# Two-block stack: the last layer's conditioning rows move into the first block's output, and a 16x16 inverse is ranked first

## The chip, the cores and the metric

One NeuronCore of a Trainium2 chip. The metric is the device time of one execution, in microseconds (us); the time given for a kernel is the median of its runs.

## The reference

The reference runs two transformer blocks one after the other, on 512 tokens and 256 context tokens of width 1024. The **first block** has one hybrid layer: a recurrent branch (RWKV-like: a state per head is decayed and updated token by token, in both directions), a latent-attention branch (MLA), a gate, an output product with `w_out` and a final norm. The **second block** has four attention layers of three kinds (a, b, c, a). Each of them is conditioned:

```python
for i in range(DEPTH_2):
    sh, sc, gt = jnp.split(jax.nn.silu(c) @ ada_w[i] + ada_b[i], 3, axis=-1)
    shc, scc, gtc = jnp.split(jax.nn.silu(c_ctx) @ ada_w[i] + ada_b[i], 3, axis=-1)
    ...
```

`c` and `c_ctx` are one row of 1024 each, and `ada_w[i]` is 1024 x 3072, so a layer's conditioning rows are a product of two rows with 12 MB of weights. They depend on nothing that the first block computes.

## The kernel before, in words

The program is written as one Python function, and a scheduler orders it: it simulates the instructions' times, and on each engine takes next what is ready and has the highest rank. Rank follows the order in the code; what is written inside `tc.high_priority()` is ranked ahead of the rest. The order that comes out is fixed: at run time every engine, and the queue of DMA issues on SyncE (SP), goes through its list in order, and an instruction whose semaphore isn't there yet holds all behind it.

Up to 460 us the first block's projections and attention run. From 460.7 to 957 us comes the recurrence (`rwkv`): six units i = 0..5, each for two directions d, in chunks of 64 or 128 tokens. A unit has a preparation (`rw_prep`), an inversion of triangular blocks (`rw_inv`) and steps (`rw_step`). In `rw_inv` the four 16x16 diagonal blocks of each 64 are taken out into D[0] (L1783, L1785), sent through DRAM into another layout (L1796 `dd<-dg`, L1802 `U<-dd`, `t<-dd`), inverted by a substitution on VectorE (DVE) that goes through 15 steps (L1810, L1811), and sent back the same way (L1815, L1816). Matrix products of 32x32 blocks (L1826, tile `psi`) make the inverse of the larger block from them. Lines L1901 (`psc`) and L1733 (`psw`) are other small products of a unit.

Between these units **fillers** run. `fillers` makes the conditioning rows of the second block's four layers with `ada_wide`: 24 loads of 512 KB a layer (L277, tile `adw`, two buffers), each followed by two matmuls of 512 columns (L279, tile `pad`; four records a load in the trace). After every eighth load a bias is added on DVE (L287, `ad_b`) and the rows go to DRAM (L288, `mods<-ad_b`). `fills` says how many loads stand behind each turn of a unit's generators: 1, 1, 2, 2, 1, 1. All 96 loads stand between 531.6 and 889.6 us.

Then `first` makes the first block's output: `gnorm` (per-head norm and gate; L1608 loads `zt`, L1650 adds a transpose on PE, L1654 makes the low half `hl` on DVE), `product(pair)` with `w_out` in three-part float32 (L192 to L194; weight loads L407, `wr`), the residual (L1974, L1975), norms, `store` (L2004 scales X on ScalarE (ACT), L2005 stores it as `xmid`) and `prep` of the second block's first layer (L683, a scaled transpose). The first projection of the second block's layer 0 is L192 into `ps`, weights `a_w_in`.

Of the kernel before, what the change touches and what calls it, by code (L numbers as in the profile page):

```python
# [15 lines left out]
AF = mybir.ActivationFunctionType  # L16
ALU = mybir.AluOpType
AX = mybir.AxisListType
# [3 lines left out]
D = 1024  # L22
# [1117 lines left out]
class Block1(Block2):  # L1140
    second = None
    ebufs = 8
    fills = 1, 1, 2, 2, 1, 1

# [435 lines left out]
    def fillers(self, adp):  # L1582

        b = self.second
        sT = self.ada_cond(adp, b["c"], b["c_ctx"], "ad", True)
        self.mds = []
        g = self.rpb_rows(adp, b["b_rpb"][0], ("adw2", 2), "ad")
        self.rpb = next(g)
        yield from g
        for l in range(4):  # L1590
            g = self.ada_wide(adp, sT, b["ada_w"][l], b["ada_b"][l], ("adw", 3), "ad")
            self.mds.append(next(g))
            yield from g
# [179 lines left out]
    def rw_inv(self, rp, d, mb):  # L1773


        nc = self.nc
        zd, zt, uo = self.zd[d]
        mq = self.mq


        D = [rp.tile([128, 8, 16], F32, tag=f"dg{d}", bufs=2, name="dg") for _ in range(3)]
        nc.vector.tensor_scalar(D[0], mb[:, :, 0:16], mq[:, 0:1], None, op0=ALU.mult)
        for q in range(1, 4):  # L1783
            nc.vector.scalar_tensor_tensor(out=D[0], in0=mb[:, :, 16 * q:16 * q + 16], scalar=mq[:, q:q + 1], in1=D[0], op0=ALU.mult, op1=ALU.add)
        c0 = 16 - 16 * d  # L1785
        nc.vector.tensor_scalar(uo[:, :, c0:c0 + 16], mb[:, :, c0:c0 + 16], mq[:, d:d + 1], None, op0=ALU.mult)
        nc.vector.scalar_tensor_tensor(out=uo[:, :, c0:c0 + 16], in0=mb[:, :, 32 + c0:48 + c0], scalar=mq[:, 2 + d:3 + d], in1=uo[:, :, c0:c0 + 16], op0=ALU.mult, op1=ALU.add)
        dd = [self.dr.tile([16, 8, 128], F32, tag=f"dd{k}", bufs=4, name=f"dd{k}") for k in range(3)]

        def rows(x):  # L1790
            return x.rearrange("s g x -> g s x")

        def blocks(x):
            return x.rearrange("s g (u t) -> (g u) s t", u=8)

        nc.sync.dma_start(out=rows(dd[0]), in_=D[0])  # L1796

        if d == 0:
            self.sub = [rp.tile([128, 16, 16], F32, tag="iv", bufs=3, name=n) for n in "UZt"]
        U, Z, tmp = self.sub  # L1800
        hs = slice(64 * d, 64 * d + 64)
        nc.sync.dma_start(out=(U, tmp)[d][hs], in_=blocks(dd[0]))  # L1802
        if d == 0:
            nc.gpsimd.memset(Z, 0.0)
            nc.gpsimd.memset(Z.rearrange("p s t -> p (s t)")[:, 0:256:17], 1.0)
        yield
        if d == 1:
            nc.vector.tensor_copy(U[hs], tmp[hs].rearrange("p s t -> p t s"))
            for n in range(1, 16):
                nc.vector.tensor_tensor(out=tmp[:, 0:n, 0:n], in0=Z[:, 0:n, 0:n], in1=U[:, 0:n, n].unsqueeze(1).to_broadcast([128, n, n]), op=ALU.mult)  # L1810
                nc.vector.tensor_reduce(out=Z[:, 0:n, n], in_=tmp[:, 0:n, 0:n], axis=AX.X, op=ALU.add)  # L1811
            nc.vector.tensor_copy(tmp, Z.rearrange("p s t -> p t s"))
        yield
        for k, src, dst, q in ((2, (tmp, Z)[d][hs], zt, nc.scalar), (1, (Z, tmp)[d][hs], zd, nc.sync)):
            q.dma_start(out=blocks(dd[k]), in_=src)  # L1815
            q.dma_start(out=D[k], in_=rows(dd[k]))  # L1816
            for e in range(2):
                nc.scalar.activation(out=dst[:, :, 16 * e:16 * e + 16], in_=D[k], func=AF.Copy, scale=self.me[:, e:e + 1])

        def wp():  # L1820
            return self.ps.tile([128, 8, 32], F32, tag=f"iv{d}", bufs=1, name="psi")

        def mm(o, out, lhsT, rhs, i=None):
            i = o if i is None else i
            for u in range(8):
                nc.tensor.matmul(out[o:o + 32, u], lhsT=lhsT[i:i + 32, u], rhs=rhs[i:i + 32, u], start=True, stop=True, tile_position=(i, o))  # L1826

        yield
        H = rp.tile([128, 8, 32], F32, tag=f"ih{d}", bufs=2, name="H")
        p = wp()  # L1830
        for r in range(0, 128, 32):
            mm(r, p, uo, zt)
        yield
        nc.vector.tensor_tensor(out=H, in0=p, in1=self.i32.unsqueeze(1).to_broadcast([128, 8, 32]), op=ALU.add)
        p = wp()
        yield
        for r in range(0, 128, 32):
            mm(r, p, H, zd)
        yield
        for r in range(0, 128, 32):  # L1840
            c0 = r % 64
            nc.scalar.copy(out=mb[r:r + 32, :, c0:c0 + 32], in_=p[r:r + 32])
        p = wp()
        hb = rp.tile([128, 8, 32], F32, tag=f"ih{d}", bufs=2, name="hb")
        for h in range(2):
            mm(64 * h + 32 * d, p, zd, H)
        yield
        tt = rp.tile([128, 8, 32], F32, tag=f"ih{d}", bufs=2, name="tt")
        for h in range(2):
            r = slice(64 * h + 32 * d, 64 * h + 32 * d + 32)  # L1850
            (nc.vector.tensor_copy, nc.scalar.copy)[h](out=tt[r], in_=p[r])
        yield
        ca, cb = 32 * d, 32 - 32 * d
        p = wp()
        for h in range(2):
            ra, rb = 64 * h + ca, 64 * h + cb
            mm(rb, p, mb[:, :, cb:cb + 32], tt, ra)
        for h in range(2):
            rb = slice(64 * h + cb, 64 * h + cb + 32)
            nc.scalar.copy(out=hb[rb], in_=p[rb])  # L1860
        p = wp()
        for h in range(2):
            ra, rb = 64 * h + ca, 64 * h + cb
            mm(ra, p, hb, mb[:, :, cb:cb + 32], rb)
        for h in range(2):
            ra = slice(64 * h + ca, 64 * h + ca + 32)
            nc.scalar.copy(out=mb[ra, :, cb:cb + 32], in_=p[ra])
# [68 lines left out]
    def first(self, sp, fx, xout, ctx_in):  # L1936
        nc, a = self.nc, self.a1
# [11 lines left out]
        rows = []  # L1949
        for i, src in enumerate((self.md[0, 2048:3072], a["final_g"])):  # L1950
            t = fx.tile([128, 1024], F32, name=f"row{i}")
# [5 lines left out]
        def product(pair):  # L1957

            tiles = pairs[pair]
            ts = slice(tiles[0], tiles[1] + 1, tiles[1] - tiles[0])  # L1960
            x = fx.tile([128, 2, 1024], F32, name=f"X{pair}")
            nc.sync.dma_start(out=x, in_=self.xpart.rearrange("(t p) n -> p t n", p=128)[:, ts])
            X[tiles[0]], X[tiles[1]] = x[:, 0], x[:, 1]
            ss = sp.tile([128, 6, 4], F32, tag="ssq", bufs=2, name="ss2")
            for nb in range(4):
                u = self.wunit(a["w_out"][0], 256 * nb, 4)
                p = self.wp2()
                for j in range(2):
                    cs = slice(128 * tiles[j], 128 * tiles[j] + 128)
                    for k in range(4):  # L1970
                        self.mm3(p[:, 256 * j:256 * j + 256], self.hh[:, k, cs], self.hl[:, k, cs], *u[k], k == 0, k == 3)
                ns = slice(256 * nb, 256 * nb + 256)
                tmp = sp.tile([128, 2, 256], F32, tag="th", bufs=2, name="yt")
                nc.vector.tensor_tensor(out=tmp, in0=p.rearrange("p (a b) -> p a b", a=2), in1=rows[0][:, :, ns], op=ALU.mult)  # L1974
                nc.vector.tensor_tensor(out=x[:, :, ns], in0=x[:, :, ns], in1=tmp, op=ALU.add)  # L1975
                if nb % 2:
                    i, hs = nb // 2, slice(256 * nb - 256, 256 * nb + 256)
                    for j in range(2):
                        self.sumsq(x[:, j, hs], ss[:, j, i:i + 1])
                    nc.vector.tensor_tensor(out=x[:, :, hs], in0=x[:, :, hs], in1=rows[1][:, :, hs], op=ALU.mult)  # L1980
                    for j in range(2):
                        self.sumsq(x[:, j, hs], ss[:, 2 + j, i:i + 1])
            xs.append(x)
            sss.append(ss)
# [16 lines left out]
        def store(pair, rst):  # L2001
# [2 lines left out]
                nc.scalar.activation(out=x[:, j], in_=x[:, j], func=AF.Copy, scale=rst[:, j:j + 1])  # L2004
            nc.sync.dma_start(out=xout.rearrange("(t p) n -> p t n", p=128)[:, tiles[0]:tiles[1] + 1:tiles[1] - tiles[0]], in_=x)  # L2005

        self.gnorm(sp, 0)
        product(0)
        self.gnorm(sp, 1)
        if self.second:  # L2010
            self.prep(sp, self.by_token(X), ssq, *self.mods, False, (4, 5))
        rst = [norms(0)]
        product(1)
        rst.append(norms(1))
        for pair in range(2):
            store(pair, rst[pair])
        self.right.close()
# [47 lines left out]
```

## Time and profile before

| | us |
|---|---|
| median of 3 runs | 2987.18 (2983.3 to 3001.24) |
| the profiled execution | 2978.0 |
| its span (first to last instruction) | 2976.0 |
| PE busy | 2695.3 (91%) |
| DVE busy | 1787.2 (60%) |

The span is one execution as the hardware profiler saw it; 2.0 us of that execution's time lie around it. Busy time of an engine is no measure of what it costs: what matters is which wait ended last. The granted clock is TensorE's, as a share of its full 2.4 GHz; 0.50 is its lower level, 1.2 GHz. Each row of a view of waits says which line's issue stood still, for whom, how long in all, how often and the longest.

### The profile page before, as it was taken

What the parts mean: (1) busy time and instruction counts of PE and PEld (TensorE: products, weight loads), DVE (VectorE), ACT (ScalarE), POOL (GpSimd) and SP (SyncE); (2) the same over time, 40 slices, a digit from 0 to 9 for tenths busy, and PEclk for the clock granted to TensorE, in tenths of its full rate; (3) what the DMA queues carried; (4) which work ended last, traced back from release to release, by engine and by line L of the source; (5) the groups of instructions that cost most, each with busy time, mean ns of one, the idle gap of its engine ahead of it and who ended that gap; (6) DMA issues with size and microseconds to landing.
All of it is one profiled execution on the core that took longest, in us unless ns stands there. A gap on an engine that the chain in (4) does not pass through costs nothing.

```text
span 2976.0 us, 55592 instructions
## 1 busy us (share of the span) xinstructions
PE 2695.3 (91%) x21935; PEld 2392.1 (80%) x21935; DVE 1787.2 (60%) x3409; ACT 1351.8 (45%) x2900; POOL 1248.4 (42%) x1328
## 2 busy tenths in 40 slices
PE   6989996899999499989989999997999998889999
PEld 4978885566668499978889899887988887788888
DVE  3344633677665636666455555546778686556675
ACT  3445631423323426556345445534545445345674
POOL 3214343264433543444534444663343244344444
PEclk8999995899995799999999999999999999999999
DMA  6143134555543211111221111322111121222112
GB/s 195 54 149 95 46 117 121 154 164 149 164 126 117 84 53 40 40 41 36 77 68 54 54 52 36 95 82 74 43 44 40 33 72 52 75 68 57 50 36 68
DMA packets 234591, 236.31 MB, mean 79 GB/s; under 512 B 57225, under 2 KB 210746, under 8 KB 234330
## 3 DMA queue, kind: packets, MB, share of 16 engines
q1 hardware_dynamic: 199616, 215.42, 24.6%
q10 hardware_dynamic: 33770, 16.29, 1.9%
q8 instruction: 172, 2.82, 0.4%
q0 software_dynamic: 944, 1.05, 0.2%
q14 instruction: 89, 0.73, 0.1%
HBM read 205.10 MB, written 28.07 MB: 78 GB/s over the span
## 4 chain that ended last, share of the span: by engine, by line
PE 66%; DVE 15%; DMA 6%; ACT 5%; issue 4%; POOL 2%; SPq 0%; ACTq 0%; DVEq 0%; POOLq 0%
PE psw L192 10%; PE psw L193 9%; PE psw L194 9%; PE psp L602 5%; PE ps L579 3%; PE psi L1826 2%; PE pad L279 2%; PE ps L580 2%; PE pso L594 2%; PE psw L1733 2%; PE psp L192 1%; PE psp L194 1%; PE psp L193 1%; DMA adw<-in_ada_w_dram 1%; DVE nm L562 1%
## 5 line engine op out<-in xcount | busy, mean ns | idle before, releaser
L185 POOL TENSOR_TENSOR wl<-wr,wh 128x512 fp32r<-128x512 f32 x362 | 477.9, 1336 | 593.7 <-ACT wh L408 482.3
L192 PE MATMUL psw<-wh,hh 128*128 128x256 f32 (+1 forms) x1888 | 546.0, 289 | 23.1 <-DVE pj L163 11.1
L194 PE MATMUL psw<-wh,hl 128*128 128x256 f32 (+1 forms) x1888 | 537.6, 285 | 1.8 <-POOL hl L185 1.8
L193 PE MATMUL psw<-wl,hh 128*128 128x256 f32 (+1 forms) x1888 | 536.6, 284 | 0.2 <-POOL wl L185 0.2
L192 PEld LDWEIGHTS psw<-wh,hh 128*128 128x128 f32 x1888 | 359.9, 191 | 33.6 <-DVE pj L163 13.6
L562 DVE TENSOR_REDUCE nm<-ps 128x1 f32<-128x768 f32 (+2 forms) x384 | 293.3, 774 | 152.0 <-PE ps L580 119.9
L194 PEld LDWEIGHTS psw<-wh,hl 128*128 128x128 f32 x1888 | 359.8, 191 | 2.8 <-POOL hl L185 2.4
L193 PEld LDWEIGHTS psw<-wl,hh 128*128 128x128 f32 x1888 | 360.2, 191 | 0.6 <-POOL wl L185 0.4
L408 ACT CAST wh<-wr 128x512 fp32r<-128x512 f32 x362 | 220.9, 617 | 248.0 <-PE psw L194 90.0
L563 ACT ACTIVATE P<-ps,nm 128x768 f32<-128x768 f32 (+1 forms) x288 | 246.8, 858 | 168.1 <-DVE nm L562 145.2
L570 DVE TENSOR_TENSOR ptl<-psp,pth 128x512 fp32r<-128x512 f32 x360 | 244.2, 686 | 128.8 <-ACT pth L569 126.4
L569 ACT CAST pth<-psp 128x512 fp32r<-128x512 f32 x360 | 207.3, 587 | 155.3 <-PE psp L602 126.0
L192 PE MATMUL psw<-hh,wh 128*128 128x512 f32 (+1 forms) x640 | 232.2, 363 | 23.2 <-DVE z L440 15.6
L193 PE MATMUL psw<-hl,wh 128*128 128x512 f32 (+1 forms) x640 | 226.5, 354 | 0.0
L194 PE MATMUL psw<-hh,wl 128*128 128x512 f32 (+1 forms) x640 | 226.3, 354 | 0.0
L579 PE MATMUL ps<-kh,qs 128*128 128x512 f32 (+1 forms) x608 | 203.1, 341 | 21.4 <-ACT P L563 14.1
L602 PE MATMUL psp<-ident,P 128*128 128x128 f32 x1408 | 218.8, 274 | 3.7 <-DVE P L1086 1.8
L580 PE MATMUL ps<-kz,qs 128*128 128x512 f32 (+1 forms) x608 | 183.4, 320 | 0.0
L602 PEld LDWEIGHTS psp<-ident,P 128*128 128x128 f32 x1408 | 164.7, 141 | 6.6 <-DVE P L1086 2.6
L192 PEld LDWEIGHTS psw<-hh,wh 128*128 128x128 f32 x640 | 122.8, 192 | 43.8 <-DVE z L440 19.7
L188 POOL TENSOR_SCALAR u<-ot 64x512 f32<-64x512 f32 x88 | 51.9, 590 | 250.8 <-ACT ot L620 247.4
L579 PEld LDWEIGHTS ps<-kh,qs 128*128 128x128 f32 x608 | 115.3, 190 | 38.8 <-ACT P L563 19.4
(509 smaller groups left out, 6645.1 us busy)
## 6 DMA issues: line engine op xcount, KB each, us to landing
adw<-in_ada_w_dram SPq DMA_DIRECT2D x96, 512.0 KB
wr<-in_a_w_in_dram SPq DMA_DIRECT2D x80, 256.0 KB
wr<-in_b_w_in_dram SPq DMA_DIRECT2D x64, 256.0 KB
wr<-in_c_w_in_dram SPq DMA_DIRECT2D x64, 256.0 KB
wr<-in_w_in_dram SPq DMA_DIRECT2D x52, 256.0 KB
adw<-in_ada_w_dram SPq DMA_DIRECT2D x48, 256.0 KB
xscr<-xt SPq DMA_DIRECT2D x36, 256.0 KB
wr<-in_a_w_out_dram SPq DMA_DIRECT2D x32, 256.0 KB
```

The costliest lines, as they stand in the source:

```text
L185: self.nc.gpsimd.tensor_tensor(out=out, in0=in0, in1=in1, op=op)
L192: mm(out, lhsT=ah, rhs=bh, start=start, stop=False)
L193: mm(out, lhsT=ah, rhs=bl, start=False, stop=False)
L194: mm(out, lhsT=al, rhs=bh, start=False, stop=stop)
L408: nc.scalar.copy(out=h, in_=raw)
L562: nc.vector.tensor_reduce(out=nm, in_=S, axis=AX.X, op=ALU.max, negate=True)
L563: nc.scalar.activation(out=dst, in_=S, func=AF.Exp, bias=nm, accum_out=l)
L569: nc.scalar.copy(out=h[:, 0:n], in_=p[:, 0:n])
L570: nc.vector.tensor_tensor(out=lo[:, 0:n], in0=p[:, 0:n], in1=h[:, 0:n], op=ALU.subtract)
L579: mm(out[:, c0:c0 + n], lhsT=qs, rhs=kh[:, k0:k0 + n], start=True, stop=False)
L580: mm(out[:, c0:c0 + n], lhsT=qs, rhs=kl[:, k0:k0 + n], start=False, stop=True)
L602: self.nc.tensor.transpose(p[:, 256 * i + 128 * t:256 * i + 128 * t + 128], P[t][:, c0 + 128 * kt:c0 + 128 * kt + 128], self.ident)
```

## The change

Two parts. First, `fills` is 1 for every unit, `fillers` makes the rows of three layers, and the fourth layer's (24 loads) are made in `first`, spread over it by `some(n)`: it computes the conditioned vector anew (`ada_cond`), uses two buffers of its own for the loads, and PSUM banks that the recurrence has left. Second, the extraction, transfers and substitution in `rw_inv` stand in `tc.high_priority()`, so their rank is first.

```diff
-    fills = 1, 1, 2, 2, 1, 1
+    fills = 1, 1, 1, 1, 1, 1
...
-        for l in range(4):
+        for l in range(3):
             g = self.ada_wide(adp, sT, b["ada_w"][l], b["ada_b"][l], ("adw", 3), "ad")
...
-        nc.vector.tensor_scalar(D[0], mb[:, :, 0:16], mq[:, 0:1], None, op0=ALU.mult)
+        with self.tc.high_priority():
+            nc.vector.tensor_scalar(D[0], mb[:, :, 0:16], mq[:, 0:1], None, op0=ALU.mult)
...
-        nc.sync.dma_start(out=rows(dd[0]), in_=D[0])
+        with self.tc.high_priority():
+            nc.sync.dma_start(out=rows(dd[0]), in_=D[0])
...
+        with self.tc.high_priority():
+            if d == 1:
+                nc.vector.tensor_copy(U[hs], tmp[hs].rearrange("p s t -> p t s"))
+                for n in range(1, 16):
...
+        fill = iter(())
+        if self.second:
+
+            b = self.second
+            sT = self.ada_cond(fx, b["c"], b["c_ctx"], "c1", True)
+            fill = self.ada_wide(fx, sT, b["ada_w"][3], b["ada_b"][3], ("adw2", 2), "c0")
+            self.mds.append(next(fill))
+
+        def some(n):
+            for _ in range(n):
+                next(fill, None)
+
         self.gnorm(sp, 0)
+        some(8)
         product(0)
+        some(4)
         self.gnorm(sp, 1)
+        some(4)
...
         rst = [norms(0)]
+        some(4)
         product(1)
         rst.append(norms(1))
+        some(4)
```

What it does to the order. On SP, the DMA issues of `first`, from the last unit's end to the first `xmid` store (`X` is the context, then each half of the residual; `row` is a broadcast gate or gain; `wr` a piece of a weight). Before:

```order
L295 DMA md_r<-mods 32x1x128
L296 DMA md_r<-in_norm_g_dram 8x128
L1945 DMA X_9745<-in_ctx_dram 128x2x1024
L1952 DMA row_9756<-mods 128x1024
L1952 DMA row_9758<-in_final_g_dram 128x1024
L1608 DMA zt<-z_d 128x4x128 x2
L1962 DMA X_9852<-xpart 128x2x1024
L407 DMA wr<-in_w_out_dram 128x2x256 x3
L1962 DMA X_10249<-xpart 128x2x1024
```

And in the change, where lines from L1785 on have other numbers (X's are L1951 and L1968, rows L1958):

```order
L407 DMA wr<-in_w_out_dram 128x2x256 x5
L1608 DMA zt<-z_d 128x4x128
L1951 DMA X_9624<-in_ctx_dram 128x2x1024
L1958 DMA row_9635<-mods 128x1024
L1958 DMA row_9637<-in_final_g_dram 128x1024
L200 DMA ad_r<-in_c_dram 8x128
L201 DMA ad_r<-in_c_ctx_dram 8x128
L277 DMA adw<-in_ada_w_dram 128x1024 x2
L282 DMA ad_b_9744<-in_ada_b_dram 2x512 x2
L1968 DMA X_9783<-xpart 128x2x1024
L1608 DMA zt<-z_d 128x4x128
L1968 DMA X_10238<-xpart 128x2x1024
```

The residual and the rows moved from ahead of all of `w_out`'s loads to behind the third `zt`, and share their place with the first `adw` loads.

SP again, around the first `xmid` store of the change (before, that store is followed by eight `wr<-in_a_w_in_dram` loads and the second store):

```order
L277 DMA adw<-in_ada_w_dram 128x1024 x3
L288 DMA mods<-ad_b_9744 2x512 x2
L282 DMA ad_b_9965<-in_ada_b_dram 2x512 x2
L277 DMA adw<-in_ada_w_dram 128x1024 x2
L2011 DMA xmid<-X_9783 128x2x1024
L277 DMA adw<-in_ada_w_dram 128x1024
L407 DMA wr<-in_a_w_in_dram 128x2x256
L277 DMA adw<-in_ada_w_dram 128x1024
L407 DMA wr<-in_a_w_in_dram 128x2x256 x3
```

Twelve of the 24 loads stand ahead of that store and twelve behind it.

On PE, the end of `first`, from the last products to layer 0's first projection (`ps`). Before:

```order
L683 MATMUL psw<-dgn,X_9852 128x128
L683 MATMUL pad<-dgn,X_9852 128x128
L683 MATMUL psw<-dgn,X_9852 128x128 x4
L683 MATMUL pad<-dgn,X_9852 128x128 x3
L683 MATMUL psw<-dgn,X_9852 128x128 x7
L192 MATMUL psw<-wh,hh 128x256
L193 MATMUL psw<-wl,hh 128x256
```

That is the prep of tiles 1 and 2, ahead of `product(1)`; no filler stands there or later. In the change, the end of `product(1)`:

```order
L194 MATMUL psw<-wh,hl 128x256
L279 MATMUL pad<-adw,ad_s 64x512 x12
L683 MATMUL psw<-dgn,X_10238 128x128
L683 MATMUL pad<-dgn,X_10238 128x128
L683 MATMUL psw<-dgn,X_10238 128x128 x5
L683 MATMUL pad<-dgn,X_10238 128x128 x3
L683 MATMUL psw<-dgn,X_10238 128x128 x6
L279 MATMUL pad<-adw,ad_s 64x512 x8
L192 MATMUL ps_10587<-wh,hh 128x256
```

Of the 24 loads of `first`, five stand ahead of the second `gnorm`'s transpose, five among the first preps, four in `product(1)`, and the last ten here: six ahead of the last prep and four behind it, all ahead of layer 0's first projection. Between the starts of the preparations of units 1, 2, 3, 4, 5 (before: 521.8, 571.4, 651.2, 720.2 and 799.7 us) and the recurrence's end, PE's list had 20, 46, 38, 42 and 46 filler matmuls, two a load; it has 20, 46, 34, 30 and 14. The last filler of the recurrence now stands at the place that ran at about 828 us before, near the start of the last unit's small products.

## Rows read from the trace of the kernel before

**Rows 1.** The page: span, and the granted clock in 40 equal slices.
```profile
span 2976.0 us, 55592 instructions
PEclk8999995899995799999999999999999999999999
```

**Rows 2.** Windows: PE, PEld, DVE, ACT, POOL busy, granted clock, DMA share, GB/s.
```profile
500.00:520.00 20.00, 20.00 (x91) 17.52 (x90) 9.22 (x20) 2.11 (x4) 5.85 (x6) 0.50 0.22 56
571.40:828.00 256.60, 242.72 (x3199) 161.82 (x3199) 187.38 (x415) 84.77 (x226) 120.53 (x144) 0.97 0.57 158
828.00:895.80 67.80, 61.76 (x798) 42.51 (x797) 48.22 (x110) 15.77 (x41) 21.58 (x22) 0.90 0.41 120
837.80:851.40 13.60, 13.60 (x98) 9.05 (x95) 8.15 (x15) 2.01 (x5) 6.62 (x5) 0.50 0.27 79
895.80:957.20 61.40, 55.42 (x836) 52.56 (x836) 30.79 (x67) 19.68 (x52) 20.05 (x19) 0.50 0.40 125
957.20:1038.60 81.40, 43.91 (x367) 42.48 (x366) 58.39 (x119) 40.00 (x80) 41.61 (x27) 0.77 0.26 84
```

**Rows 3.** The same windows for L279 alone: PE, PEld, granted clock, DMA share, GB/s.
```profile
571.40:828.00 256.60, 81.72 (x280) 16.44 (x280) 0.97 0.57 158
828.00:895.80 67.80, 19.30 (x64) 3.54 (x64) 0.90 0.41 120
837.80:851.40 13.60, 4.91 (x12) 0.88 (x12) 0.50 0.27 79
895.80:957.20 61.40, 0.00 (x0) 0.00 (x0) 0.50 0.40 125
```

**Rows 4.** Chain of waits by line: 571.4 to 828 us, then 828 to 895.8.
```profile
by line: PE pad L279 17.7%; PE psi L1826 14.3%; PE psw L1733 9.5%; DMA adw<-in_ada_w_dram 6.6%; DVE t L1810 5.3%; DMA dg<-dd 4.3%; DMA dd<-Z 4.1%; DMA t<-dd 3.1%; DVE Z L1811 3.1%; PE psc L1901 2.8%; issue 2.7%; DMA dd<-t 2.4%; PE psw L1753
...
by line: PE pad L279 21.2%; PE psi L1826 20.3%; PE psw L1733 13.9%; PE psc L1901 5.3%; DVE t L1810 5.2%; DVE bk L1719 5.1%; DVE R L1921 3.8%; PE psw L1767 3.5%; DVE ad_b L287 3.0%; PE psw L1753 3.0%; DVE Z L1811 2.7%; DVE y L1931 2.3%; issu
```

**Rows 5.** Pieces of the chain, 520 to 960 us: start, us, what.
```profile
667.52 2.88 DMA dd<-t
684.53 1.93 PE psc L1901 x16
739.60 4.96 DMA dd<-Z
876.30 1.91 PE psi L1826 x64
899.14 3.65 PE psc L1901 x16
921.59 7.06 PE psi L1826 x160
```

**Rows 6.** SP's issues in `first`: start us, us from first to last, what.
```profile
903.00 0.41 SPq L1945 DMA_DIRECT2D X<-in_ctx_dram  x1
956.68 3.22 SPq L1608 DMA_DIRECT2D zt<-z_d  x2
963.09 20.48 SPq L407 DMA_DIRECT2D wr<-in_w_out_dram  x8
1004.48 0.37 SPq L2005 DMA_DIRECT2D xmid<-X  x1
1007.31 16.04 SPq L407 DMA_DIRECT2D wr<-in_a_w_in_dram  x8
```

**Rows 7.** SP's waits, 571.4 to 895.8 us: us in all, times, longest.
```profile
SPq L277 <- PE pad L279: 143.9, 68, 9.5
SPq L277 <- DMA adw<-in_ada_w_dram: 33.1, 32, 2.5
SPq L288 <- DVE ad_b L287: 23.6, 20, 8.0
```

**Rows 8.** Timelines of DVE and PE in `first`: idle before, and releaser, in brackets.
```profile
961.74 0.69 DVE L1974 TENSOR_TENSOR yt<-pad,row 128x512 f32<-128x512 f32 x1 [2.22 <-PE pad L194]
...
1026.54 0.77 PE L683 MATMUL psw<-dgn,X 128*128 128x128 f32 x2 [11.73 <-issue]
...
1038.64 0.58 PE L192 MATMUL ps<-wh,hh 128*128 128x256 f32 x1 [5.53 <-DVE one L1053]
```

More of the change, by code (lines that the diff above doesn't have):

```diff
@@ L1781, in rw_inv @@
         D = [rp.tile([128, 8, 16], F32, tag=f"dg{d}", bufs=2, name="dg") for _ in range(3)]
-        nc.vector.tensor_scalar(D[0], mb[:, :, 0:16], mq[:, 0:1], None, op0=ALU.mult)
-        for q in range(1, 4):
-            nc.vector.scalar_tensor_tensor(out=D[0], in0=mb[:, :, 16 * q:16 * q + 16], scalar=mq[:, q:q + 1], in1=D[0], op0=ALU.mult, op1=ALU.add)
+        with self.tc.high_priority():
+            nc.vector.tensor_scalar(D[0], mb[:, :, 0:16], mq[:, 0:1], None, op0=ALU.mult)
+            for q in range(1, 4):
+                nc.vector.scalar_tensor_tensor(out=D[0], in0=mb[:, :, 16 * q:16 * q + 16], scalar=mq[:, q:q + 1], in1=D[0], op0=ALU.mult, op1=ALU.add)
         c0 = 16 - 16 * d
@@ L1801, in rw_inv @@
         hs = slice(64 * d, 64 * d + 64)
-        nc.sync.dma_start(out=(U, tmp)[d][hs], in_=blocks(dd[0]))
+        with self.tc.high_priority():
+            nc.sync.dma_start(out=(U, tmp)[d][hs], in_=blocks(dd[0]))
         if d == 0:
@@ L1806, in rw_inv @@
         yield
[L1807 to L1812, printed above, removed]
-        yield
[L1814 to L1818, printed above, removed]
+        with self.tc.high_priority():
+            if d == 1:
+                nc.vector.tensor_copy(U[hs], tmp[hs].rearrange("p s t -> p t s"))
+                for n in range(1, 16):
+                    nc.vector.tensor_tensor(out=tmp[:, 0:n, 0:n], in0=Z[:, 0:n, 0:n], in1=U[:, 0:n, n].unsqueeze(1).to_broadcast([128, n, n]), op=ALU.mult)
+                    nc.vector.tensor_reduce(out=Z[:, 0:n, n], in_=tmp[:, 0:n, 0:n], axis=AX.X, op=ALU.add)
+                nc.vector.tensor_copy(tmp, Z.rearrange("p s t -> p t s"))
+        yield
+        with self.tc.high_priority():
+            for k, src, dst, q in ((2, (tmp, Z)[d][hs], zt, nc.scalar), (1, (Z, tmp)[d][hs], zd, nc.sync)):
+                q.dma_start(out=blocks(dd[k]), in_=src)
+                q.dma_start(out=D[k], in_=rows(dd[k]))
+                for e in range(2):
+                    nc.scalar.activation(out=dst[:, :, 16 * e:16 * e + 16], in_=D[k], func=AF.Copy, scale=self.me[:, e:e + 1])
         def wp():
```

## Prediction

> **What bounds the kernel now.** I read the page's clock line first. Of 40 slices of the span nearly all stand at the full clock; the dips lie in the first 14 slices, the recurrence among them [rows 1]. The layers behind 1038.6 us keep their work in the change, so I looked only at what lies ahead. The windows say what limits each stretch [rows 2]. From 571.4 to 828 us PE is busy 242.72 of 256.60 us: 95%, at clock 0.97. So a matmul taken out there is worth nearly its time. From 957.2 to 1038.6 us PE is busy only 43.91 of 81.40 us, and DVE 58.39: this is where the change puts the last layer's rows, and 37.5 us of idle PE stand ready for them. But one stretch warns against a simple sum: from 895.8 to 957.2 us, still in the recurrence, PE is busy 55.42 of 61.40 us and the granted clock is 0.50, the lower level of 1.2 GHz. The view of the fillers alone shows what differs: no filler runs there [rows 3].
>
> Next, what feeds the fillers. In 256.6 us 280 records, so 70 loads, were worked off: 3.67 us for a load of 512 KB, at 158 GB/s in all [rows 2, 3]. SP's waits say why not faster: it stood 143.9 us for the matmuls that read the buffer two loads earlier, and 33.1 us for the earlier load itself [rows 7]. Two buffers and SP's order set the pace, and the change keeps two.
>
> **The change, part by part.** The sum is made against the profiled execution, 2978.0 us, which is 2976.0 of span and 2.0 around it; the median of the runs shown, 2987.18, lies 9.2 above it, and I add the sum to that.
>
> *Eight loads out of the third and fourth preparation.* Their fillers go from 38 and 42 matmuls to 34 and 30, so 8 loads go. On the chain of waits from 571.4 to 828 us the fillers' matmuls have 17.7% and their loads 6.6%, so 45.4 and 16.9 us, and by 70 loads 0.89 us each [rows 4]. PE alone counts 81.72 / 70 = 1.17 a load. The load's wait goes too, since the loads left have more time. 8 x 0.89 = **-7** (-9 by PE's time, 0 if other waits fill the place).
>
> *Sixteen loads out of the last unit.* All lie behind 828 us, where 64 filler records took 19.30 us of PE [rows 3], and 21.2% of 67.8 us of chain, 14.4 us [rows 4]. At an unchanged clock that is 16 x 0.90 = -14. The other end: the clock falls as the fillers end. Without fillers PE's work there is 61.76 - 19.30 = 42.5 us, of which 13.60 - 4.91 = 8.7 run at 0.50 already [rows 2, 3], so 33.8 us are at the full clock. The same products at both levels: 16 of L1901 take 1.93 and 3.65 us, a ratio of 1.89; those of L1826 30 ns each (64 in 1.91 us) and 44 ns (160 in 7.06), 1.48 [rows 5]; 1.69 between them. That adds 33.8 x 0.69 = 23 us, so 65.8 of work and the 6.0 idle as before make 71.8, against 67.8: +4. Which end? The nearest row is the same unit's own end, where PE is 90% busy without fillers at 0.50; and from 500 to 520 us, with no filler either, PE is busy 20.00 of 20.00 us at 0.50 [rows 2]. Both say that these small products don't hold the clock by themselves. The last filler ran to 889.6, and the low stretch begins at 895.8: I count as much behind the last filler as warm, 6 us that don't grow by the share of 0.69 / 1.69 = 0.41, 2.4 us. I take **+2**, and keep -14 and +4.
>
> The Trainium skill ("TensorE: Matmul & The Clock Gate", section "HAM oscillation — how this bites in real kernels") speaks of a clock that falls where PE idles for a load between groups of matmuls, and of keeping PE fed as the cure. By that the last unit, with fewer waits for loads, would stay warm and the sum would be the second rival's. The trace does not agree: 20.00 of 20.00 us busy, at 0.50.
>
> *The ranking.* In the order hardly a row moves: the substitution already stood nearly by itself on DVE, and on SP the two transfers become neighbours where loads stood between. What it can give is a transfer that isn't behind a 512 KB load: 2.88 us for `dd<-t` against 4.96 for `dd<-Z` [rows 5], 2.1 us once a unit, six times 12. What it can cost is DVE work of other units pushed behind 15 steps; PE is 95% busy and has other work then. I take **-3**, between -12 and +3 (a quarter of 12 on the other side).
>
> *The rows in `first`.* Its 24 loads need 24 x 3.67 = 88 us at the old pace. The first is issued behind the third `zt`, which waits for DVE and comes at 956.68 [rows 6], and behind X and the rows; then `w_out`'s eight loads, which take SP until 963.09 + 20.48 = 983.6, stand between the `adw` loads. Half of the 24 stand behind the first `xmid` store, which in the trace is issued at 1004.48 [rows 6] and can't come earlier. From there 12 loads at 3.67 us, or at the 3.3 of the best stretches (an estimate: a tenth less than the mean), end at 1044 to 1049; the last load still has to land and be multiplied (its 1.2 us, and 2 to 3 of flight); two pairs of `mods` stores wait for DVE on SP, 23.6 / 20 = 1.2 us each time and up to 8.0 [rows 7]. Then PE's list lets layer 0's first projection go, at 1038.64 before [rows 8]. That is 1045 to 1066, and my middle 1054: +16. There is also the way through the last prep: six loads stand ahead of its L683, at 1026.54 before. The eighth load behind the store ends at 1004.5 + 8 x 3.67 + 3 = 1037, so the prep is 10 us later and layer 0 too, at 1049; less than 1054, so it doesn't add.
>
> The residual and the rows, issued at 903 before [rows 6], come behind 956.68, while DVE's L1974 read `row` at 961.74 [rows 8]. DVE waits some 4 us there, and PE's second `gnorm` transpose with it. It is covered by the loads' own delay above; with fewer loads it would itself be the cost. PE's 28 us of fillers (24 x 1.17) fit in the 37.5 idle. In return PE is kept at work where the clock was 0.77 [rows 2]: of 43.9 us of matmuls, some 8 at the low level lie on the path (the last prep, layer 0's first products at 0.41 us [rows 8]), worth 3. So `first` is **+13** (between +6 and +28).
>
> Nothing else has a price: the added conditioned vector is two 4 KB loads and one transpose in a PE that idles, and the third layer's rows are not read before the layers are well under way.
>
> Sum: -7 + 2 - 3 + 13 = **+5**, 2983 in a profile like this one, 2992 as a median.
>
> **The rivals.**
> *Forecast* (chance 0.50): a small change in either direction, about 2992; by its terms' bounds 2980 to 3003.
>
> *The clock holds in the last unit* (0.27). Then -7 - 14 - 3 and, with loads at the quick pace, +6: -18, 2969; with all of the ranking's 12, 2960. For it: the low stretch at 837.8 to 851.4 us fell though 12 filler records lay in it [rows 3], so fillers are not all that decides; the unit's order changes. Against it: the two windows without fillers.
>
> *`first` becomes a queue of loads* (0.18, the slower side). Mechanism: SP issues in order; 12 `adw` loads, eight `wr` of `a_w_in` and the `mods` stores alternate behind the `xmid` store, each `adw` waits for the matmuls two loads earlier, and PE holds layer 0 behind the last. It decides from the point where a load's turn is above 3.67 us or the store is later than 1009. With +28 there, +4 in the last unit and no ranking: -7 + 4 + 28 = +25, 3012. For it: 4 MB of X and rows come into the same stretch, behind which the first `adw` loads wait. Against it: the mean there was 84 GB/s, so there is room.
>
> *The ranking does more or less than said* (0.05): +9 or -3 on the forecast, within its range.
>
> About 1%, 30 us, is what a measurement of this kernel can tell from no change. Faster by over 1% needs both the clock and the ranking: 0.07. Slower by over 1% needs the queue at its worst, and DVE's late rows on top: 0.10. Within: 0.83. The range, to hold 8 in 10, goes from the clock's case to the queue's: 2964 to 3014.
>
> **What would show it.** In the new profile: granted clock behind the recurrence's last filler at 0.50 for the rest of the unit (right) or 0.9 and more (the second case); start of `first`'s products 5 to 10 us earlier than 956.5 against 20 or more; the first `ps` projection of layer 0 about 13 us later, counted from that start; SP's waits for `pad` in `first` as long as in the recurrence; `dd<-Z` transfers near 2.9 us if the ranking pays. The prediction is wrong if the projection waits for something other than the last loads, or if the layers behind it take other times than before.

## The result, and the profile after

The change is **slower**: ratio 1.0101 to the kernel before, 95% interval 1.0078 to 1.0124, so +23 to +37 us. The medians of four runs each are 3022.85 (3017.35 to 3027.8) and 2985.24 (2980.85 to 3001.24), 37.6 us apart, at the upper end of that interval. The forecast was 2992, from 2964 to 3014. The profiled execution took 3027.8 us.

The page's span and clock line, after:

```profile
span 3026.0 us, 55606 instructions
PEclk8999995797865899999999999999999999999999
```

Against [rows 1] three more slices inside the recurrence stand below 9. The windows of the change (columns as in [rows 2]) for three stretches, which the rest of this text uses for every kernel: the recurrence from the end of its first low stretch to the first product of the output; the output, up to layer 0's first projection; the layers. The fourth row is the recurrence's end.

```profile
525.00:976.40 451.40, 409.03 (x5093) 306.78 (x5092) 289.97 (x656) 132.63 (x350) 175.31 (x201) 0.77 0.39 104
976.40:1075.90 99.50, 76.25 (x466) 47.20 (x465) 64.32 (x129) 43.27 (x90) 38.28 (x28) 0.81 0.70 239
1075.90:3026.00 1950.10, 1802.67 (x13509) 1690.71 (x13507) 1212.66 (x2221) 959.47 (x2002) 854.63 (x877) 0.97 0.19 55
916.00:976.40 60.40, 52.93 (x830) 50.20 (x826) 29.50 (x59) 14.28 (x35) 19.31 (x19) 0.53 0.14 43
```

The same stretches in the kernel before, in the execution that the prediction used:

```profile
522.00:956.50 434.50, 402.35 (x5189) 282.51 (x5189) 298.71 (x664) 135.75 (x360) 176.97 (x201) 0.87 0.52 146
1038.60:2976.00 1937.40, 1794.29 (x13507) 1681.84 (x13507) 1208.12 (x2218) 959.27 (x2003) 856.00 (x878) 0.98 0.19 56
```

The reader is to see this: in the recurrence PE has 96 records fewer, and yet is busy 409.0 us where it was 402.4, at a clock of 0.77 where it was 0.87. The output is 99.5 us, where it was 1038.6 - 956.5 = 82.1 (a row of it is in [rows 2]). Of the 50.0 us between the two spans 3.0 lie ahead of the recurrence, 16.9 in it, 17.4 in the output and 12.7 in the layers.

What fills the output's 99.5 us is in its lists. SP's issues there, parts of the list from the third `zt` to just ahead of the second store (L numbers as in the change; columns as in [rows 6]):

```profile
976.54 0.37 SPq L1608 DMA_DIRECT2D zt<-z_d  x1
977.50 0.47 SPq L1958 DMA_DIRECT2D row<-mods  x1
979.47 0.83 SPq L277 DMA_DIRECT2D adw<-in_ada_w_dram  x2
993.74 1.21 SPq L277 DMA_DIRECT2D adw<-in_ada_w_dram  x2
...
1030.81 0.38 SPq L2011 DMA_DIRECT2D xmid<-X  x1
1033.83 0.33 SPq L277 DMA_DIRECT2D adw<-in_ada_w_dram  x1
...
1059.99 9.65 SPq L277 DMA_DIRECT2D adw<-in_ada_w_dram  x4
```

DVE's first row of the output, and PE's last rows ahead of layer 0, as in [rows 8]:

```profile
983.81 0.69 DVE L1980 TENSOR_TENSOR yt<-pad,row 128x512 f32<-128x512 f32 x1 [5.09 <-DMA row<-mods]
```

```profile
1067.34 1.94 PE L279 MATMUL pad<-adw,ad_s 128*64 128x512 f32 x8
1072.06 3.95 PE L279 MATMUL pad<-adw,ad_s 128*64 128x512 f32 x8 [2.79 <-DMA adw<-in_ada_w_dram]
1075.94 0.58 PE L192 MATMUL ps<-wh,hh 128*128 128x256 f32 x1
```

Loads are issued from 979.47 to 1069.6: 24 in 90 us, 3.76 each; the twelve behind the first store take 38.8 us, 3.2 each. Layer 0's first projection starts when the last one's matmuls end, with no idle time between.

### The profile page after: what moved, and what is told of

It reads as the page before. It is cut to its first block, busy times and chain, and to the rows that moved or that the text cites. A ratio compares the mean times of both kernels' runs of the same rounds, so it can differ in the third digit from the quotient of the medians.

```text
span 3026.0 us, 55606 instructions
## 1 busy us (share of the span) xinstructions
PE 2746.3 (91%) x21936; PEld 2432.5 (80%) x21936; DVE 1788.5 (59%) x3412; ACT 1353.1 (45%) x2901; POOL 1242.2 (41%) x1328
## 5 line engine op out<-in xcount | busy, mean ns | idle before, releaser
L192 PE MATMUL psw<-hh,wh 128*128 128x512 f32 (+1 forms) x640 | 231.8, 362 | 23.4 <-DVE z L440 15.5
L279 PE MATMUL pad<-adw,ad_s 128*64 128x512 f32 x384 | 128.2, 748 | 33.3 <-DMA adw<-in_ada_w_dram 29.7
```

Of the source, the lines that this page charges most:

```text
L192: mm(out, lhsT=ah, rhs=bh, start=start, stop=False)
```

## The experiments

Each kernel was compared with the kernel before on the same chip, whose medians there were 2992.69 (first four kernels), 2992.70 (next four) and 2995.56. In tables, "recurrence", "output" and "layers" are the three stretches above.

**Which part of the change costs?** The move alone, the ranking alone, the change with matmuls that keep PE at work, and the change without the last layer's rows.

*e1*: `rw_inv` as before, the rest as in the change.

> The move of the last layer's rows alone, the inversion ranked as before. Clock theory (the recurrence lost about 17 us because fewer fillers leave its small products at the lower clock, and the first block's output another 17 because of its loads; the ranking does nothing): as the change, 3015 to 3030. Rival, ranking theory (substitution and transfers ranked first push other work aside, and that is what the recurrence lost): the recurrence gets its 17 us back, 3000 to 3010.

*e2*: the kernel before with the change's `rw_inv`.

> The ranking alone; all four layers' rows stay in the recurrence at the old rate. Clock theory: as the kernel before, 2978 to 2995, clock in 571 to 828 us above 0.95. Ranking theory: 2997 to 3008, the loss in the units' stretches with the clock as before.

*e3*: the change, and in `fillers`, behind the three layers:

```diff
+        for k in range(24):
+            p = self.ps.tile([128, 512], F32, tag="ad", bufs=1, name="pad")
+            for j in range(2):
+                nc.tensor.matmul(p[64 * j:64 * j + 64], lhsT=sT[:, k % 8], rhs=self.w2, ...)
+            yield
```

> The change plus 24 pairs of matmuls without loads (the operand is the resident w2, the result is read by nobody) behind the recurrence's last filler, so where the change took 16 loads' matmuls away. It adds 28 us of PE work. Clock theory: the low stretches at 839 to 870 and 891 to 955 us shrink, and the recurrence ends 5 to 15 us earlier in spite of the added work: 3005 to 3018. Rival, work theory (the recurrence is bound by PE's work or by waits of another kind, and the clock is a by-product): 10 to 28 us later, 3033 to 3050.

*e4*: in `first`, `self.mds.append(self.mds[2])` in place of `ada_cond` and `ada_wide`.

> The change without the last layer's rows: layer 3 takes layer 2's rows, and the first block's output has no filler. Loads theory (the output's extra 17 us are its 24 loads): the output is back at 80 to 84 us, so 3003 to 3010, and the recurrence as long as in the change. Rival (the output is longer because X and the rows are issued late): the output stays over 90 us, 3013 to 3025.

| | ratio (95%) | recurrence | output | layers |
|---|---|---|---|---|
| change | 1.0101 (1.0078 to 1.0124) | 451.4 | 99.5 | 1950.1 |
| e1, move alone | 1.0007 (0.9986 to 1.0028) | 427.5 | 97.3 | 1938.8 |
| e2, ranking alone | 1.0070 (1.0040 to 1.0100) | 469.6 | 79.9 | 1954.5 |
| e3, matmuls added | 1.0072 (1.0044 to 1.0100) | 456.4 | 92.5 | 1939.4 |
| e4, no last rows | 1.0029 (1.0011 to 1.0047) | 449.0 | 80.4 | 1948.4 |

My first theory fell. I had put the recurrence's loss down to the missing fillers alone; but the move alone costs nothing that can be seen, and the ranking alone +12 to +30 us. Both totals lie beyond even what the rival gave (2992.91, below its 3000 to 3010, and 3014.43, above its 2997 to 3008). e3 was to gain 5 to 15 us in the recurrence; in its profile that is 5 us longer, though its clock there is 0.82 and not 0.77. Its total, 3015.25, lies inside what the clock theory gave and outside the rival's: some 28 us of work (by the price of a load's matmuls) were added, and the time did not grow beyond the change's. So on top of the ranking the missing fillers do count.

The output is 80.4 us again without the last layer's rows (the total, 3000.82, is just under the 3003 to 3010 expected). But e4 can't divide the loads from its rival, the late residual and rows: with the loads gone, SP issues X and the rows early again, as in the kernel before (e4, SP). e10, further below, divides them: its rows come late, DVE waits even longer for them (e10, DVE), and with eight loads its output takes 83.2 us, against 97.3 with 24 in e1. So the late rows cost little by themselves, and the other sixteen loads make the rest.

```profile
907.49 0.41 SPq L1951 DMA_DIRECT2D X<-in_ctx_dram  x1
907.95 0.46 SPq L1958 DMA_DIRECT2D row<-mods  x1
```

```profile
970.79 0.69 DVE L1975 TENSOR_TENSOR yt<-pad,row 128x512 f32<-128x512 f32 x1 [6.49 <-DMA row<-mods]
```

**What in the ranking costs?** The windows of the recurrence in e1 and e2:

```profile
525.40:952.90 427.50, 387.17 (x5076) 289.20 (x5075) 284.17 (x644) 130.98 (x346) 171.57 (x199) 0.81 0.40 108
```

```profile
523.80:993.40 469.60, 431.38 (x5187) 301.08 (x5185) 294.38 (x664) 135.17 (x358) 176.73 (x201) 0.79 0.49 135
```

e2 has the work of the kernel before, and DVE and ACT are as busy (294 and 135 us against 299 and 136): nothing was added. PE is 29 us busier with the same number of matmuls, at a lower clock. One stretch shows it best. PE's timeline in e2 behind a unit's substitution, where the clock is at 0.50 for 40.9 us:

```profile
682.66 0.62 PE L1832 MATMUL psi<-zd,zd 32*32 32x32 f32 x14 [0.17 <-ACT zd L1824]
683.47 0.43 PE L1907 MATMUL psc<-R,x 128*128 128x64 f32 x2 [0.19 <-DVE R L1927]
683.72 0.30 PE L1692 MATMUL psw<-lt,sel 128*128 128x128 f32 x1
683.93 2.42 PE L1907 MATMUL psc<-R,x 128*128 128x64 f32 x14
686.28 1.98 PE L279 MATMUL pad<-adw,ad_s 128*64 128x512 f32 x4
688.19 0.90 PE L1692 MATMUL psw<-lt,sel 128*128 128x128 f32 x3
689.02 4.43 PE L1832 MATMUL psi<-zd,zd 32*32 32x32 f32 x102
693.38 1.98 PE L279 MATMUL pad<-adw,ad_s 128*64 128x512 f32 x4
695.28 0.85 PE L1832 MATMUL psi<-zd,zd 32*32 32x32 f32 x12
696.06 1.98 PE L279 MATMUL pad<-adw,ad_s 128*64 128x512 f32 x4
697.96 5.73 PE L1832 MATMUL psi<-zd,H 32*32 32x32 f32 x128
703.62 3.68 PE L279 MATMUL pad<-adw,ad_s 128*64 128x512 f32 x8
707.23 3.06 PE L1832 MATMUL psi<-H,zd 32*32 32x32 f32 x64
710.22 2.08 PE L1733 MATMUL psw<-x,bk 128*128 128x128 f32 x8
```

Two windows of e2, this low stretch and the whole unit from one substitution's end to the next:

```profile
684.90:725.80 40.90, 40.90 (x467) 27.55 (x466) 17.17 (x32) 12.66 (x37) 9.31 (x10) 0.50 0.35 104
674.20:767.00 92.80, 87.92 (x925) 58.32 (x921) 56.75 (x128) 23.14 (x63) 35.85 (x45) 0.76 0.44 124
```

PE's timeline in the kernel before, at the same place of the program:

```profile
677.45 1.91 PE L1826 MATMUL psi<-zd,zd 32*32 32x32 f32 x64 [1.82 <-ACT zd L1818]
681.08 3.45 PE L279 MATMUL pad<-adw,ad_s 128*64 128x512 f32 x8 [1.73 <-issue]
684.46 2.00 PE L1901 MATMUL psc<-R,x 128*128 128x64 f32 x16
686.38 0.90 PE L1826 MATMUL psi<-zd,zd 32*32 32x32 f32 x26
687.22 1.08 PE L279 MATMUL pad<-adw,ad_s 128*64 128x512 f32 x4
688.23 0.99 PE L1826 MATMUL psi<-zd,zd 32*32 32x32 f32 x32
```

Four records of L279 take 1.08 us at the full clock and 1.98 at the low one. In the kernel before, behind 64 small products and a fall of the clock (3.45 us for eight records), come fillers and wide products, and the clock is back by 687. In e2 the two directions' 32x32 products come together, in groups of 102, 128 and 64 with only fillers between them, and L1733 after them. PE shows no idle time in those 40.9 us, and its clock stays at 0.50; in the 6.9 us ahead of them it idled 1.3 us. Wide matmuls are not missing there: 32 filler records take 15.5 of the 40.9 us, and eight in a row at 703.62 raise nothing.

That gave a theory in two steps: the ranking groups the 32x32 products on PE, and with such groups the clock, once fallen, stays low. Its rival was work displaced on DVE, ACT or SP. Five more kernels: the three parts of the ranking each alone on the kernel before (e5, e6, e7), the ranking with added matmuls ahead of each first group (e8), and the kernel before with the products themselves ranked, with DVE's one addition between them, and nothing else (e9).

> The kernel before with the extraction of the diagonal blocks and its transfers (dd<-dg, U and t<-dd) ranked first, nothing else. Theory 'clock' (the ranking costs because the scheduler then puts the 32x32 products of both directions together behind the substitution, ahead of the wider ones, and they follow a fall of the clock without raising it): no such group arises from this part alone, so as before within 8 us, 2985 to 3000. Rival 'displaced work' (work of the other direction waits behind ranked DVE work): +5 at most here.

> The kernel before with the substitution on DVE alone ranked first. Clock theory: as before within 8 us, since the PE order keeps its short groups. Displaced work: this is the part with the most DVE work, so the whole +15 to +22, with the clock as before.

> The kernel before with the result transfers and the zd activations alone ranked first. Clock theory: this is the part that brings the 32x32 products forward, but without the earlier extraction the two directions stay apart: 0 to +10. Displaced work: 0, ACT has room.

> The ranking alone, plus six matmuls of 128x128 by 256 columns (their result is overwritten) ahead of each direction's first 32x32 products, so behind each substitution: 72 of them, about 30 us of PE work. Clock theory: the long low stretch at 685 to 726 us becomes shorter than 15 us, the time from that substitution's end to the next falls from 92.8 to 75 to 85 us in spite of the added work, and the total stays at 3000 to 3018. Displaced work: the stretch grows by the added 5 us, and the total goes to 3035 to 3045.

> The kernel before with none of the change's ranking; instead the inverse's first two 32x32 products of each direction (L1826, tile psi) are ranked first, so PE takes them in whole groups of 64 as soon as they can start. Order theory (what costs is that these products stand in groups ahead of the wider ones, where the clock has fallen): the low time in the units grows, and the total goes up by 10 to 30, 3003 to 3023. Rival (the ranked transfers, substitution or copies themselves cost, by what they push aside on SP, DVE and ACT): as before within 8 us.

The edit of e8, in `rw_inv` ahead of the first products, and of e9 (the next two steps of the inverse stand in such blocks too):

```diff
+        for _ in range(6):
+            nc.tensor.matmul(p.rearrange("p u t -> p (u t)"), lhsT=zd...[:, 0:128], rhs=self.w2[:, 0:256], start=True, stop=True)
...
+        with self.tc.high_priority():
+            p = wp()
+            for r in range(0, 128, 32):
+                mm(r, p, uo, zt)
```

Last, the kernel before again (e12), for a second profile of one program.

> The kernel before once more, for a second profile: how far do the stretches of one program differ between executions? If the recurrence's 495.8 us (460.7 to 956.5) comes back within 5 us, the differences of 17 to 35 us between kernels are the kernels' own; the layers behind (1937 us) are expected to differ by up to 15.

The recurrence's windows of e12 and e9:

```profile
522.00:970.40 448.40, 414.89 (x5188) 291.49 (x5187) 295.58 (x664) 135.04 (x358) 174.93 (x201) 0.84 0.51 142
```

```profile
521.00:994.70 473.70, 436.08 (x5191) 304.62 (x5190) 296.84 (x664) 136.57 (x360) 176.58 (x201) 0.79 0.48 134
```

The windows of e8, the recurrence and the unit shown above, and its added matmuls (a group of the costliest: busy us, mean ns):

```profile
520.40:998.50 478.10, 435.72 (x5333) 307.34 (x5331) 296.73 (x664) 135.17 (x359) 178.28 (x201) 0.88 0.47 133
677.70:751.60 73.90, 69.42 (x823) 45.68 (x822) 54.30 (x117) 20.26 (x56) 28.11 (x32) 0.95 0.58 163
```

```profile
L1838 PE MATMUL psi<-w,zd 128*128 128x256 f32 x144 | 38.9, 418 | 3.3 <-DVE R L1929 2.0 <-ACT zd L1824 1.4
```

From a windows row the low time follows as (1 - clock) x 2 x length, and what it costs is 0.41 of it, by the prediction's ratio of 1.69. The rest of the stretch is idle time of PE and work as it would be at the full clock (estimates; the rounding of the clock is worth 4 to 5 us of low time either way):

| recurrence | ratio (95%) | length | low time | its cost | PE idle | work |
|---|---|---|---|---|---|---|
| before | | 434.5 | 113 | 46 | 32 | 356 |
| e12, before again | | 448.4 | 143 | 59 | 34 | 356 |
| e5, extraction ranked | 0.9985 (0.9954 to 1.0015) | 429.9 | 103 | 42 | 32 | 355 |
| e6, substitution ranked | 1.0027 (0.9999 to 1.0056) | 440.2 | 123 | 51 | 34 | 355 |
| e7, results ranked | 1.0051 (1.0021 to 1.0081) | 456.7 | 146 | 60 | 42 | 355 |
| e2, all three | 1.0070 (1.0040 to 1.0100) | 469.6 | 197 | 81 | 38 | 351 |
| e9, products ranked | 1.0100 (1.0062 to 1.0137) | 473.7 | 199 | 82 | 38 | 355 |
| e8, ranking and burst | 1.0110 (1.0064 to 1.0155) | 478.1 | 115 | 47 | 42 | 389 |
| e1, move alone | 1.0007 (0.9986 to 1.0028) | 427.5 | 162 | 67 | 40 | 321 |
| change | 1.0101 (1.0078 to 1.0124) | 451.4 | 208 | 85 | 42 | 324 |

The column of work says that no kernel with 96 loads in the recurrence has more to do, but for e8's added matmuls. What differs is the clock's cost, and in second place 4 to 10 us of idle time. e9 decides for the order: with no transfer, substitution or copy ranked, it has e2's low time and no smaller loss (3026.45 us, above the 3003 to 3023 expected). Its groups are those of e2's kind:

```profile
684.00 5.72 PE L1826 MATMUL psi<-zd,zd 32*32 32x32 f32 x114 [0.22 <-ACT zd L1818]
695.16 6.47 PE L1826 MATMUL psi<-zd,H 32*32 32x32 f32 x128
```

e8 decides for the clock: the same ranking with PE's burst has the low time of the kernel before again (115 against 197 us), and the unit shown above, from substitution's end to substitution's end, takes 73.9 us in place of 92.8. But its 38.9 us of added matmuls cost what the clock gave back, so the total, forecast at 3000 to 3018, is 3026.78, though still below the 3035 to 3045 of the rival: evidence for the clock, no remedy. It does not say what brought the clock back, since the burst also broke up the groups. In e8's unit the products stand like this:

```profile
699.65 1.03 PE L1832 MATMUL psi<-zd,zd 32*32 32x32 f32 x32
700.61 1.08 PE L279 MATMUL pad<-adw,ad_s 128*64 128x512 f32 x4
701.62 0.62 PE L1832 MATMUL psi<-zd,zd 32*32 32x32 f32 x14
```

Of the parts, the extraction costs nothing measurable, the results most (+6 to +24 us; its profile shows this as 8 us of idle time, at e12's low time), the substitution perhaps 8 us (its interval just touches 1); the three ratios add up to 1.006, about what all three cost together. The medians of e6 and e7, 12 and 11 us above the kernel before, lie a little beyond the 8 and 10 that the clock theory allowed them.

e12 missed its expectation: the same program's recurrence came out 13.9 us longer, by these estimates nearly all of it low clock, and the execution took 2997.05 us. So a difference under some 15 us between single profiles can't be called a kernel's own; the verdicts rest on the ratios, and on low times that lie 54 us and more above e12's.

Every execution's span and mean granted clock were kept too, which gives a low time over the whole span for each of them (estimates again). In the 31 executions of the kernel before beside e1 to e4 it goes from 322 to 392 us and the time from 2979.91 to 3014.08, with 0.40 us of time to each us of low time (correlation 0.91): most of one program's spread is its clock, and the price of 0.41 holds. As medians, each against the kernel before beside it: e2 389 against 347 us, e9 411 against 359, e8 333 against 353, e5, e6 and e7 350, 369 and 369 against 353. At 0.41 the clock makes 17 of e2's +21 us and 21 of e9's +30; of e6 and e7 it makes some 7 us each, and the rest of e7's +15 is waiting. The change has 435, the move alone 365 and e3 365.

**A version that is better than both?** e10 moves only the last 8 of layer 3's loads (`ada_wide` gets a range of columns) and ranks nothing; e11 adds the extraction's ranking.

> No ranking, fills as before; only the last 8 of layer 3's 24 loads are moved into the first block's output, the other 16 stay in the recurrence. By the terms measured: 8 loads less in the recurrence -3 to -7, the output 0 to +4, since all eight stand ahead of the first xmid store: 2985 to 2993, the ratio 0.997 to 1.000. Rival (any load in the output delays DVE's first rows by 4 us and more, and the whole output with it): +5 to +10.

> The eight loads moved, and of the ranking only the extraction with its transfers. If the two add: ratio 0.995 to 0.999. If the scheduler's order is upset by any ranking together with the move: 1.002 or more.

Both came out as expected. e10: 0.9984 (0.9962 to 1.0006), no difference shown; its output takes 83.2 us. e11: 0.9970 (0.9944 to 0.9996), median 2990.85 against 2995.56: 0.3% faster than the kernel before, hardly clear of noise, and the only one that is.

## Why the prediction was wrong

**The ranking** is the step that failed. I took -3, between -12 and +3, and the rival set on it went no further than 9 above the forecast; alone it costs 0.4 to 1.0%, +12 to +30 us. "In the order hardly a row moves" was read from DVE's and SP's lists, where the ranked instructions stand. What moved was PE's: its 32x32 products of both directions form groups, and the clock stays low longer; that makes some 17 of +21 us in e2 (an estimate, from the low times above). In a stretch where PE is 95% busy its list was the one to read. And I had the price in hand: [rows 5] show the small products 1.5 times, others 1.9 times as long at the low clock, but I used this only for the fillers' removal. Nor had I a term for the two parts of the change together: alone they add up to 1.0077, the change measured 1.0101, and its low time over the span, 435 us, is 88 above the 347 of the kernel before, where the parts have 18 and 42 more.

**The loads taken out of the recurrence** (-7 and +2): the move alone shortens it by 7 us against the profile used and by 21 against e12's. The sign of the sum was right, the size cannot be had closer than that spread. The end of the recurrence did run at the low level, as forecast (0.53 in the change's fourth row, 0.59 from 846 us on, some 5 us behind the last filler).

**The rows in `first`** (+13, between +6 and +28): +15.2 in e1, +17.4 in the change against 82.1, and gone without the loads and the late rows (e4). Mechanism as forecast: 3.76 us a load, layer 0 behind the last load, DVE's first rows 5.09 us late. The terms were off in both directions. The store comes 54.4 us after the first product (48.0 before), so the twelve loads behind it started 6 us later than I had counted; layer 0 comes 45.1 us behind the store, where my middle had 49.5. And the 3 us that I took off for a warmer PE did not come: the last eight filler records take 3.95 us, against 1.94 for the eight before them, and the granted clock from 1072.0 to 1077.5 us is 0.50. The 0.41 us that I gave there for layer 0's first products does not stand in [rows 8].

With the ranking left out, the sum was +8, and the move alone measured -4 to +8. So two of the change's three places and their mechanisms stood, and the third, set aside as small, decided. **The slower rival** gave a time of 3012 through the loads and came nearest in time, but by another mechanism: it counted on no loss by the ranking. Of its two conditions one came, a store later than 1009 (956.5 + 54.4 = 1010.9 on the old scale), and the other, a load's turn above 3.67 us, did not where it was to count (3.2 us behind the store). **What would show it**: I asked for the output to start 5 to 10 us earlier, or 20; it started 19.9 us later, which was the sign that the recurrence had been misjudged. The layers taking another time was a sign of error too, and they did (1950.1 against 1937.4).

The base was off too: the profile I summed against has 113 us of low time in the recurrence, the second one of the same program 143.

Left open: the layers took 1937 to 1944 us in the kernel before and 1948 to 1955 in e2, e4 and the change, but 1939 in e1 and e3. e10 and e11, which are no slower than the kernel before, have 1948 and 1952, so the length does not follow the loss. Summed over windows of 10 us, the layers' low time is 81 us in the profile used, 97 in e12, and 102 to 108 in e2, e4, the change, e10 and e11, which at 0.41 covers 9 to 11 of the 11 to 17 us: the execution's clock, as far as is known, but not separated from the kernel's. Nor was it tried why the clock stays low with groups of small products and comes back with a mixed order, nor whether in e8 it was the added matmuls or the broken groups that brought it back.

## What to carry to other kernels

A priority on one engine's work can change the lists of all: after ranking anything, read first the list of the engine that bounds the stretch, even if nothing of it was ranked. Where matmuls of very different size share PE, their order can be worth something by itself: here grouping the small ones cost some 17 to 21 us of clock (e2, e9). And take two profiles of the kernel before, ahead of a sum whose terms are smaller than their difference; the mean granted clock of every execution tells how far a profile is a typical one.

## What was not expected of the hardware

PE fully busy does not mean a full clock: 40.90 us busy of 40.90, at 0.50 throughout, in e2. The Trainium skill ("TensorE: Matmul & The Clock Gate", section "HAM oscillation — how this bites in real kernels") tells of falls where PE idles for loads; here PE had idled 1.3 us in the 6.9 us ahead of the fall, but not while the clock stayed low, and in e8 the low time shrank with matmuls added and no wait taken away (PE idle 42 us in the recurrence, 38 in e2). One program's low time in the recurrence differed by 30 us between two executions, and its length by 13.9; over 31 executions the time went with the low time of the span at 0.40 us for each us.
